# Forgetting attention in a hybrid block: token blocks handled in fours instead of pairs, row tiles of their own width, and a smaller GpSimd DMA scratch

## The chip, the cores and the metric

The kernel runs on one core of one Trainium2 chip. The metric is the device time of one execution in microseconds. The time before is 1698.5 us, the median of three runs (1698.43 to 1699.84). All arithmetic is on 32-bit floats; matrix products use the form `float32r`, in which an operand is split into a rounded high part and the rest, and one product becomes two or three matrix instructions.

## The reference, cut to what matters

One layer of a streaming encoder on 1024 tokens of width 1024: a gated linear recurrence (HGRN2), forgetting attention (FoX), cross-attention into 256 memory tokens, a gated merge, and a feed-forward mixer. The change lies in the forgetting attention alone, eight heads of 64 channels:

```python
s = (jnp.einsum('bhqd,bhkd->bhqk', qh[:, :, lo:hi], kh[:, :, :hi]) * scale
     + Fc[:, :, lo:hi, None] - Fc[:, :, None, :hi])
mask = (lo + jnp.arange(Q_BLOCK))[:, None] >= jnp.arange(hi)[None, :]
p = jax.nn.softmax(jnp.where(mask, s, -jnp.inf), axis=-1)
outs.append(jnp.einsum('bhqk,bhkd->bhqd', p, vh[:, :, :hi]))
```

Here `lo:hi` is one of eight blocks of 128 query tokens. Block `tb` looks at the `tb + 1` key blocks up to its own; its own one is masked to a triangle. `Fc` is a running sum of log forget gates.

## The kernel before, in words

The program is one long stream per engine, and its stages follow each other: input projections and gates, cross-attention, forgetting attention, HGRN2, merge, feed-forward. Python generators yield after each step, and `weave` mixes several of them by shares. The order on each engine is then fixed at build time by a planner that plays the program through on modelled times (`schedule_with_timeline_sim=True`); `ahead` raises the priority of what a generator emits by 300. On the chip each engine carries out its list in that fixed order.

**Forgetting attention** is `fox_attn` (from L901), called for each of four pairs `p` of heads and each head `i` of the pair. It is woven with work that fills TensorE meanwhile: the projection of the next pair (`fox_proj`, 256 columns a matmul) for `i = 0`, chunks of the gates (`gates_early`, 512 columns) for `i = 1`, and for the last pair HGRN2's values and then HGRN2's first projections (`hgrn_prep`). A head does its eight query blocks in four pairs `tp`:

- For each of the two blocks: two matmuls per piece of up to 512 keys into the PSUM tile `lg` (L924, L925), VectorE adds the bias and takes the row maximum (L930), ScalarE takes the exponential and its sum (L940), VectorE the reciprocal (L941), GpSimd scales the row (L942). The result is `pt`, of which there are four buffers of 1024 columns.
- Then, for two key blocks at a time, four (or three) 128x128 transposes (L953, L954, L956) fill one of two PSUM banks `tr`. `split` makes the high part `ph` on ScalarE (L166) and the rest `pl` on VectorE (L174), two buffers each. Per key block one matmul with `ph` (L965) and one with `pl` (L966) follow, both with the values `vhl` as weights, into the PSUM bank `po`, of which there is one. They have 256 columns (both query blocks), or 128 for the key block that only the second query block sees.
- At the end of a pair of blocks ScalarE copies the lower half of `po` (L969), VectorE adds the upper half (L970), and SyncE's queue writes `yp` to HBM (L971).

`fox_proj` squares its projections into `fsq` (L857 to L859), which for pairs after the first takes one of the four `pt` buffers. All these tiles are in the pool `pf`, which lies in the place of the cross-attention's pool and is followed in the same place by HGRN2's pool `ph` (`open_hgrn`).

GpSimd issues 128 DMAs in the run: some weights (`rw`, L595 and L1457), sums of weights made by accumulating DMAs (L1522, L1523), and a few others. For the descriptors of these DMAs the program reserves a scratch in each SBUF partition, whose size is a parameter of the program (L1804); where it isn't given, as here, it is 16384 bytes.

Of the kernel before, what the change touches and what calls it, by code (L numbers as in the profile page):

```python
# [8 lines left out]
F32 = mybir.dt.float32  # L9
F32R = mybir.dt.float32r  # L10
AF = mybir.ActivationFunctionType
ALU = mybir.AluOpType
AX = mybir.AxisListType

P = 128
T = 1024
D = 1024
KC = D // P
HB = 512
# [19 lines left out]
FOX_STEPS, HGRN_STEPS, MEM_STEPS = 28, 14, 7  # L39
AHEAD = 300  # L40
FOX_LATE = 0.2
SEQ = ("w0 x0 s0 w1 x1 s1 w2 x2 s2 w3 x3 s3 w4 x4 s4 x5 s5 x6 s6 x7 s7 u0 u1 u2 u3 mn u4 u5 u6 u7 lk k0 k1 k2 k3 lx "
       "q0 me k4 q1 k5 c0 ly c1 lz q2 q3 k6 q4 q5 k7 d0 q6 q7 xn d1 mv cv f1 f2 f3 du ev mk").split()
WFIRST = {0: (0, 1), 1: (1, 2), 2: (2, 3), 3: (3, 4), 4: (4, 8)}
# [47 lines left out]
def run_all(gen):  # L92
    for _ in gen:
        pass
# [15 lines left out]
def tile_block(ctx: ExitStack, tc: tile.TileContext, xT, memT, x_rows, mem_rows, vec, fbias, mats, hmask, w_first, w_cm, w_hi, w_fqk, w_fv,  # L110
               w_mkv, w_br, w_out, w_up, w_dn, w_pair, outT):
    nc = tc.nc
    V, S, G, PE, SP = nc.vector, nc.scalar, nc.gpsimd, nc.tensor, nc.sync
# [25 lines left out]
    ident = cp.tile([P, P], F32, tag="ident", name="ident")  # L139
# [24 lines left out]
    def cast(eng, out, in_):  # L164
        if eng is S:
            return S.copy(out, in_)  # L166
        elif eng is V:
            return V.tensor_copy(out, in_)
        else:
            return G.tensor_scalar(out, in_, 1.0, 0.0, ALU.mult, ALU.add)  # L170

    def split(eng, h, l, src, sub=None):
        late["split cast"] = cast(eng, h, src)
        return (sub or V).tensor_sub(l, src, h.bitcast(F32))  # L174
# [64 lines left out]
    pt = Rounded(tc, name="pt", bufs=1, side="right")  # L239
# [212 lines left out]
    ybd = tc.dram_tile([P, 4, T], F32, name="ybd")  # L452
# [165 lines left out]
    named = dict(du=first_unit, f1=families_step, f2=families_step, f3=families_step, mn=mem_norm, me=keys_out, mk=mem_keys, mv=mem_values, xn=x_norm, lk=load_late, lx=lambda: load_rows(*T2[2:], *T1[2:]), ly=lambda: load_rows(*T2[:2]), lz=lambda: load_rows(*T2[2:]), ev=first_gates, cv=first_cover)  # L618
    for what in SEQ:
        if what in named:  # L620
# [101 lines left out]
    pm = Rounded(tc, name="pm", bufs=1, side="right", reuse_waits="tile")  # L722
    pools = {}
# [120 lines left out]
    def fox_proj(p):  # L844

        fox_z[p] = [None, None]

        def evac(tb, ps):
            n, b = tb // 4, tb % 4
            if b == 0:  # L850
                fox_z[p][n] = pq.tile([P, 4, 256], F32, tag="z", name=f"z{p}_{n}", bufs=2)
            z = fox_z[p][n]
            S.activation(z[:, b, :], ps, AF.Copy, scale=rt[:, tb:tb + 1])
            if b == 3:
                zz = z.rearrange("p b (h d) -> p (b h) d", d=64)
                sq = pools["pf"].tile([P, 16, 64], F32, tag="pt", name="fsq", bufs=4) if p else \
                    pm.tile([P, 16, 64], F32, tag="fsq", name="fsq")  # L857
                r = cp.tile([P, 16], F32, tag="fr", name="fr", bufs=2)
                S.activation(sq, zz, AF.Square)  # L859
                V.reduce_sum(r, sq, axis=AX.X)  # L860
                rstd_small(r, r, 64)
                V.tensor_mul(zz, zz, r.unsqueeze(2).to_broadcast([P, 16, 64]))

        yield from token_major(w_fqk[p], 256, evac)
# [36 lines left out]
    def fox_attn(p, i):  # L901
        kh, kl, qa, _ = fox_sets[p]
        h = 2 * p + i
        a = slice(64 * i, 64 * i + 64)
        if h not in fox_vh:
            fox_vsplit(h)
        vhl = fox_vh[h]
        nf = pf.tile([P, T], F32, tag="nf", name="nf")
        SP.dma_start(nf, negFd[h:h + 1, :].partition_broadcast(P))
        for tp in range(4):  # L910
            pts = []
            for j in range(2):
                tb = 2 * tp + j
                ns = (tb + 1) * P
                tsl = slice(tb * P, (tb + 1) * P)
                pt = pf.tile([P, T], F32, tag="pt", name="pt", bufs=4)
                st = pf.tile([P, 4], F32, tag="st", name="st", bufs=4)
                nfm = pf.tile([P, P], F32, tag="nfm", name="nfm")
                G.tensor_tensor(nfm, nf[:, tsl], mskf, ALU.add)
                m = 0  # L920
                for s0 in range(0, ns, HB):
                    w = min(HB, ns - s0)
                    ps = ps_lg()
                    PE.matmul(ps[:, :w], qa[i][:, tsl], kh[i][:, s0:s0 + w], start=True, stop=False)  # L924
                    fox_sets[p][3] = PE.matmul(ps[:, :w], qa[i][:, tsl], kl[i][:, s0:s0 + w], start=False, stop=True)  # L925

                    d = w - P if s0 + w == ns else w
                    for lo, hi, bias in ((0, d, nf[:, s0:s0 + d]), (d, w, nfm)):
                        if lo < hi:
                            V.tensor_tensor_reduce(out=pt[:, s0 + lo:s0 + hi], in0=ps[:, lo:hi], in1=bias,  # L930
                                                   op0=ALU.add, op1=ALU.max, scale=1.0, scalar=-3e38,
                                                   accum_out=st[:, m:m + 1])
                            m += 1
                if m == 3:
                    V.tensor_tensor(st[:, 0:1], st[:, 0:1], st[:, 2:3], ALU.max)
                if m > 1:
                    V.tensor_scalar(st[:, 2:3], st[:, 0:1], st[:, 1:2], -1.0, ALU.max, ALU.mult)  # L937
                else:
                    V.tensor_scalar(st[:, 2:3], st[:, 0:1], -1.0, None, ALU.mult)
                S.activation(pt[:, :ns], pt[:, :ns], AF.Exp, bias=st[:, 2:3], accum_out=st[:, 3:4])  # L940
                V.reciprocal(st[:, 3:4], st[:, 3:4])  # L941
                G.tensor_scalar(pt[:, :ns], pt[:, :ns], st[:, 3:4], 0.0, ALU.mult, ALU.add)  # L942
                pts.append(pt)
                yield
            po = ps_po()
            for sp in range(tp + 1):
                ptr = ps_tr()
                w = 384 if sp == tp else 512
                for jj in range(2):
                    sb = 2 * sp + jj  # L950
                    ssl = slice(sb * P, (sb + 1) * P)
                    if sb <= 2 * tp:
                        PE.transpose(ptr[:, jj * 256:jj * 256 + P], pts[0][:, ssl], ident)  # L953
                        PE.transpose(ptr[:, jj * 256 + P:jj * 256 + 256], pts[1][:, ssl], ident)  # L954
                    else:
                        PE.transpose(ptr[:, 256:384], pts[1][:, ssl], ident)  # L956
                ph = pf.tile([P, HB], F32R, tag="ph", name="ph", bufs=2)
                pl = pf.tile([P, HB], F32R, tag="pl", name="pl", bufs=2)
                split(S, ph[:, :w], pl[:, :w], ptr[:, :w])
                for jj in range(2):  # L960
                    sb = 2 * sp + jj
                    last = sb == 2 * tp + 1
                    o = po[:, P:256] if last else po[:, 0:256]
                    src = slice(256, 384) if last else slice(jj * 256, jj * 256 + 256)
                    PE.matmul(o, vhl[:, sb, :], ph[:, src], start=(sb == 0), stop=False)  # L965
                    PE.matmul(o, vhl[:, sb, :], pl[:, src], start=False, stop=last)  # L966
                yield
            yp = pf.tile([64, 256], F32, tag="yp", name="yp")
            S.copy(yp, po[64:128, :256])  # L969
            V.tensor_add(yp, po[0:64, :256], yp)  # L970
            SP.dma_start(ybd[a, p, tp * 256:(tp + 1) * 256], yp)  # L971
            yield

    weave((chain(fox_values(), fox_proj(0)), 25), (ahead(memory(), AHEAD), 4 * MEM_STEPS))
# [1 line left out]
    pf = pools["pf"] = Rounded(tc, name="pf", bufs=1, side="right", reuse_waits="tile")  # L976
# [4 lines left out]
    for p in range(3):  # L981
        weave((ahead(fox_attn(p, 0), AHEAD), FOX_STEPS), (fox_proj(p + 1), 8))
        fox_prep(p + 1, fox_sets[p][3])
        weave((ahead(fox_attn(p, 1), AHEAD), FOX_STEPS), (gates_early(NFOX[2 * p + 1]), 2 * NFOX[2 * p + 1], FOX_LATE))

# [246 lines left out]
    for i in range(2):  # L1232
        weave((ahead(fox_attn(3, i), AHEAD), FOX_STEPS), (islice(values, 8), 8),
              (gates_early(0 if i else NFOX[6]), 2 * NFOX[6], FOX_LATE))
    run_all(values)
# [96 lines left out]
    pl = Rounded(tc, name="pl", bufs=1, side="right", reuse_waits="tile")  # L1332
# [39 lines left out]
    for i, j in enumerate((0, 4, 1, 5, 2, 6, 3, 7)):  # L1372
        chunk = cm_chunk(w_out[j], KC, mh, ml, i == 7)
        if i == 7:
            sum7 = pu.tile([P, T], F32, tag="rx", name="sum7")
            first = next(chunk)
            begun = first_operands()
            chunk = chain((first,), chunk)
        for n, ps in chunk:
# [10 lines left out]
            else:  # L1390
                sq = sqs[:, sl]
# [152 lines left out]
    for p in range(NF // 2):  # L1544
# [32 lines left out]
        for i in range(2):  # L1577
            f = 2 * p + i
            c = pq.tile([P, T], F32, tag="fc", name="fc", bufs=4)
            w = [col(C_CW + t * NF + f) for t in range(3)]  # L1580
# [88 lines left out]
    for a, b, own, first, c, n, sign, last, xq in (  # L1669
# [9 lines left out]
        for i, ks in enumerate(steps):  # L1679
# [11 lines left out]
            for m in range(4):  # L1691
# [6 lines left out]
                if ks.stop == NP:  # L1698
                    j, sl = m + 4 * c, slice(n * HB, (n + 1) * HB)
# [115 lines left out]
```

## Time and profile before

| What | Value |
|---|---|
| Median of three runs | 1698.5 us (1698.43 to 1699.84) |
| The profiled execution's own time | 1700.23 us |
| Its span in the trace | 1698.4 us |
| Granted TensorE clock | 0.999 |
| Instructions in the trace | 24291, of them 8957 matmuls |
| Forgetting attention's stage | from about 324 us to 681 us of the span |

The span reaches from the first to the last instruction of the program; the execution's own time is 1.8 us longer. In the rows below, `PE` is a matmul on TensorE, `PEld` the load of its weights, `DVE` VectorE, `ACT` ScalarE, `POOL` GpSimd. A row of groups gives a line of the kernel, the engine, the operation, output and inputs, shapes and the count, then the busy time in us and the mean duration in ns, and last the idle time before. A row of a timeline gives start and duration in us. A row of windows gives the busy time and, as (x...), the count of instructions that lie in or reach into the window.

### The profile page before, as it was taken

Reading aid. Unit: us, or ns where it says so; the run is one execution under the profiler, and the core shown is the slowest. Engines: PE = TensorE matmul, PEld = TensorE weight load, DVE = VectorE, ACT = ScalarE, POOL = GpSimd, SP = SyncE. Lnnn points to the kernel's source line nnn. Section 1 sums busy time; section 2 is a strip of 40 time slices with the busy share of each in tenths; the row PEclk is TensorE's granted clock in tenths of the full one; section 3 lists DMA queues with packets and bytes.
Section 4 is the critical chain, followed back from the end, with each engine's and each line's share of the span. In section 5 each row is a group of like instructions: output and inputs, shape, how many; then the busy total and the mean of one; then the engine's idle time right before and its main releaser. Section 6 shows DMA issues by size and latency. Waiting matters only on the chain.

```text
span 1698.4 us, 24291 instructions
## 1 busy us (share of the span) xinstructions
PE 1691.0 (100%) x8957; PEld 1452.4 (86%) x8957; DVE 1150.8 (68%) x2057; ACT 800.9 (47%) x1428; POOL 324.6 (19%) x420
## 2 busy tenths in 40 slices
PE   9999999999999999999999999999999999999999
PEld 7888899989898998888888888888888888888887
DVE  6966455666666664886856845987878888775654
ACT  6734455545454553775631333644434444533432
POOL 0200032543433331544310000311111111100000
PEclk9999999999999999999999999999999999999999
DMA  9443232221212111110346542566544344494772
GB/s 367 157 161 106 88 139 68 77 92 51 94 59 77 63 46 57 67 32 13 106 127 209 167 186 100 165 174 169 158 139 138 118 149 143 172 363 145 251 269 87
DMA packets 83062, 227.16 MB, mean 134 GB/s; under 512 B 9712, under 2 KB 12408, under 8 KB 82816
## 3 DMA queue, kind: packets, MB, share of 16 engines
q1 hardware_dynamic: 64320, 160.54, 26.8%
q0 software_dynamic: 18048, 64.50, 13.2%
q8 instruction: 70, 1.15, 0.3%
q10 hardware_dynamic: 576, 0.59, 0.1%
q14 instruction: 48, 0.39, 0.1%
HBM read 180.72 MB, written 67.93 MB: 146 GB/s over the span
## 4 chain that ended last, share of the span: by engine, by line
PE 99%; DVE 0%; ACT 0%; DMA 0%; issue 0%; ACTq 0%; DVEq 0%
PE pp L160 21%; PE pp L162 21%; PE pp L161 21%; PE lg L160 4%; PE lg L162 4%; PE lg L161 4%; PE tr L162 3%; PE tr L161 3%; PE tr L160 3%; PE po L966 1%; PE lg L925 1%; PE lg L924 1%; PE po L965 1%; PE po L160 1%; PE po L161 1%; PE po L162 1%
## 5 line engine op out<-in xcount | busy, mean ns | idle before, releaser
L160 PE MATMUL pp<-uh,wh 128*128 128x512 f32 x412 | 163.3, 396 | 0.0
L161 PE MATMUL pp<-ul,wh 128*128 128x512 f32 x412 | 162.9, 395 | 0.0
L162 PE MATMUL pp<-uh,wl 128*128 128x512 f32 x412 | 162.5, 394 | 0.0
L161 PE MATMUL pp<-wl,uh 128*128 128x256 f32 (+1 forms) x512 | 146.3, 286 | 0.0
L162 PE MATMUL pp<-wh,ul 128*128 128x256 f32 (+1 forms) x512 | 146.1, 286 | 0.0
L160 PE MATMUL pp<-wh,uh 128*128 128x256 f32 (+1 forms) x512 | 145.6, 286 | 0.0
L166 ACT CAST wh<-s 128x512 fp32r<-128x512 f32 x110 | 66.5, 621 | 131.6 <-PE pp L161 55.1
L166 ACT CAST wh<-raw 128x1024 fp32r<-128x1024 f32 (+2 forms) x76 | 67.6, 890 | 100.6 <-PE pp L161 86.2
L166 ACT CAST wh<-rw 128x512 fp32r<-128x512 f32 x87 | 53.2, 619 | 108.1 <-PE pp L161 70.2
L160 PEld LDWEIGHTS pp<-wh,uh 128*128 128x128 f32 x512 | 97.3, 190 | 1.2
L161 PEld LDWEIGHTS pp<-wl,uh 128*128 128x128 f32 x512 | 97.4, 190 | 1.0
L162 PEld LDWEIGHTS pp<-wh,ul 128*128 128x128 f32 x512 | 97.4, 190 | 0.9
L1457 POOL DMA_DIRECT2D rw<-in_w_up x44 | 24.1, 555 | 372.4 <-DVE wl L1350 171.3
L166 ACT CAST dwh<-wr 128x1024 fp32r<-128x1024 f32 (+1 forms) x41 | 40.2, 980 | 115.8 <-PE tr L161 40.0
L162 PEld LDWEIGHTS pp<-uh,wl 128*128 128x128 f32 x412 | 77.5, 188 | 15.1
L174 DVE TENSOR_TENSOR wl<-raw,wh 128x1024 fp32r<-128x1024 f32 (+2 forms) x75 | 78.0, 1040 | 17.8 <-ACT wh L166 17.6
L160 PEld LDWEIGHTS pp<-uh,wh 128*128 128x128 f32 x412 | 77.5, 188 | 14.6
L161 PEld LDWEIGHTS pp<-ul,wh 128*128 128x128 f32 x412 | 77.5, 188 | 14.5
L940 ACT ACTIVATE pt<-pt,st 128x128 f32<-128x128 f32 (+3 forms) x64 | 49.7, 777 | 41.7 <-DVE st L937 33.9
L174 DVE TENSOR_TENSOR dwl<-wr,dwh 128x1024 fp32r<-128x1024 f32 (+1 forms) x41 | 46.3, 1129 | 31.7 <-ACT dwh L166 31.7
L942 POOL TENSOR_SCALAR pt<-pt,st 128x128 f32<-128x128 f32 (+3 forms) x64 | 49.1, 767 | 78.4 <-DVE st L941 64.1
L1350 DVE TENSOR_TENSOR wl<-rw,wh 128x512 fp32r<-128x512 f32 x69 | 47.7, 704 | 22.7 <-PE pp L162 18.2
(500 smaller groups left out, 5123.2 us busy)
## 6 DMA issues: line engine op xcount, KB each, us to landing
rw<-in_w_up POOLq DMA_DIRECT2D x44, 512.0 KB, 4.7
sd<-in_w_dn POOLq DMA_DIRECT2D x30, 512.0 KB, 6.0
br<-yd SPq DMA_DIRECT2D x30, 512.0 KB, 5.0
raw<-in_w_cm SPq DMA_DIRECT2D x24, 512.0 KB, 3.4
gd<-gt SPq DMA_DIRECT2D x48, 256.0 KB, 2.0
gt<-gd SPq DMA_DIRECT2D x48, 256.0 KB, 2.7
yd<-fc SPq DMA_DIRECT2D x44, 256.0 KB, 2.2
wr<-sd SPq DMA_DIRECT2D x20, 512.0 KB, 4.5
```

The costliest lines, as they stand in the source:

```text
L160: PE.matmul(ps, lh, rh, start=first, stop=False, skip_group_check=more)
L161: PE.matmul(ps, lh, rl, start=False, stop=False, skip_group_check=more)
L162: return PE.matmul(ps, ll, rh, start=False, stop=last, skip_group_check=more)
L166: return S.copy(out, in_)
L174: return (sub or V).tensor_sub(l, src, h.bitcast(F32))
L924: PE.matmul(ps[:, :w], qa[i][:, tsl], kh[i][:, s0:s0 + w], start=True, stop=False)
L925: fox_sets[p][3] = PE.matmul(ps[:, :w], qa[i][:, tsl], kl[i][:, s0:s0 + w], start=False, stop=True)
L940: S.activation(pt[:, :ns], pt[:, :ns], AF.Exp, bias=st[:, 2:3], accum_out=st[:, 3:4])
L942: G.tensor_scalar(pt[:, :ns], pt[:, :ns], st[:, 3:4], 0.0, ALU.mult, ALU.add)
L965: PE.matmul(o, vhl[:, sb, :], ph[:, src], start=(sb == 0), stop=False)
L1350: late["split"] = V.tensor_sub(l, src, h.bitcast(F32))
L1457: late["raw"] = G.dma_start(raw[:, 2 * i:2 * i + 2, :], src[:, 2 * i:2 * i + 2, :])
```

## The change

A head does its eight query blocks in two groups `g` of four. The rows of the eight blocks get eight tiles `pt0` to `pt7`, each of the width that the block needs (128 to 1024 columns, one buffer each), in place of four buffers of 1024. For one key block at a time, up to four transposes fill a PSUM bank, one for each query block of the group that sees this key block; one split and two matmuls of 512, 384, 256 or 128 columns follow. `ph` and `pl` have three buffers (`PARTS`). The end of a group copies and adds 512 columns. `fsq` gets a tile of its own. GpSimd's DMA scratch is set to 4096 bytes.

```diff
-                sq = pools["pf"].tile([P, 16, 64], F32, tag="pt", name="fsq", bufs=4) if p else \
-                    pm.tile([P, 16, 64], F32, tag="fsq", name="fsq")
+                sq = (pools["pf"] if p else pm).tile([P, 16, 64], F32, tag="fsq", name="fsq")
...
-        for tp in range(4):
+        for g in range(2):
             pts = []
-            for j in range(2):
-                tb = 2 * tp + j
+            for tb in range(4 * g, 4 * g + 4):
...
-                pt = pf.tile([P, T], F32, tag="pt", name="pt", bufs=4)
+                pt = pf.tile([P, ns], F32, tag=f"pt{tb}", name=f"pt{tb}")
...
             po = ps_po()
-            for sp in range(tp + 1):
+            for sb in range(4 * g + 4):
                 ptr = ps_tr()
-                w = 384 if sp == tp else 512
-                for jj in range(2):
-                    sb = 2 * sp + jj
-                    ssl = slice(sb * P, (sb + 1) * P)
-                    if sb <= 2 * tp:
-                        PE.transpose(ptr[:, jj * 256:jj * 256 + P], pts[0][:, ssl], ident)
-                        PE.transpose(ptr[:, jj * 256 + P:jj * 256 + 256], pts[1][:, ssl], ident)
-                    else:
-                        PE.transpose(ptr[:, 256:384], pts[1][:, ssl], ident)
-                ph = pf.tile([P, HB], F32R, tag="ph", name="ph", bufs=2)
-                pl = pf.tile([P, HB], F32R, tag="pl", name="pl", bufs=2)
-                split(S, ph[:, :w], pl[:, :w], ptr[:, :w])
-                for jj in range(2):
-                    sb = 2 * sp + jj
-                    last = sb == 2 * tp + 1
-                    o = po[:, P:256] if last else po[:, 0:256]
-                    src = slice(256, 384) if last else slice(jj * 256, jj * 256 + 256)
-                    PE.matmul(o, vhl[:, sb, :], ph[:, src], start=(sb == 0), stop=False)
-                    PE.matmul(o, vhl[:, sb, :], pl[:, src], start=False, stop=last)
+                first = max(sb - 4 * g, 0)
+                for j in range(first, 4):
+                    PE.transpose(ptr[:, j * P:(j + 1) * P], pts[j][:, sb * P:(sb + 1) * P], ident)
+                ph = pf.tile([P, HB], F32R, tag="ph", name="ph", bufs=PARTS)
+                pl = pf.tile([P, HB], F32R, tag="pl", name="pl", bufs=PARTS)
+                c = slice(first * P, HB)
+                split(S, ph[:, c], pl[:, c], ptr[:, c])
+                PE.matmul(po[:, c], vhl[:, sb, :], ph[:, c], start=sb == 0, stop=False)
+                PE.matmul(po[:, c], vhl[:, sb, :], pl[:, c], start=False, stop=sb == 4 * g + 3)
                 yield
...
-    nc = bacc.Bacc("TRN2", target_bir_lowering=False, num_devices=1)
+    nc = bacc.Bacc("TRN2", target_bir_lowering=False, num_devices=1, dynamic_dma_scratch_size=4096)
```

More of the change, by code (lines that the diff above doesn't have):

```diff
@@ L41 @@
 FOX_LATE = 0.2
+PARTS = 3
 SEQ = ("w0 x0 s0 w1 x1 s1 w2 x2 s2 w3 x3 s3 w4 x4 s4 x5 s5 x6 s6 x7 s7 u0 u1 u2 u3 mn u4 u5 u6 u7 lk k0 k1 k2 k3 lx "
@@ L939, in fox_attn @@
                     V.tensor_scalar(st[:, 2:3], st[:, 0:1], -1.0, None, ALU.mult)
-                S.activation(pt[:, :ns], pt[:, :ns], AF.Exp, bias=st[:, 2:3], accum_out=st[:, 3:4])
+                S.activation(pt, pt, AF.Exp, bias=st[:, 2:3], accum_out=st[:, 3:4])
                 V.reciprocal(st[:, 3:4], st[:, 3:4])
-                G.tensor_scalar(pt[:, :ns], pt[:, :ns], st[:, 3:4], 0.0, ALU.mult, ALU.add)
+                G.tensor_scalar(pt, pt, st[:, 3:4], 0.0, ALU.mult, ALU.add)
                 pts.append(pt)
@@ L967, in fox_attn @@
+                PE.matmul(po[:, c], vhl[:, sb, :], pl[:, c], start=False, stop=sb == 4 * g + 3)
                 yield
[L968 to L971, printed above, removed]
+            yp = pf.tile([64, HB], F32, tag="yp", name="yp")
+            S.copy(yp, po[64:128, :])
+            V.tensor_add(yp, po[0:64, :], yp)
+            SP.dma_start(ybd[a, p, g * HB:(g + 1) * HB], yp)
```

## The prediction

> **What bounds the kernel now.** I read the page's busy times first, then the chain of work that ended last.
>
> ```profile
> span 1698.4 us, 24291 instructions
> PE 1691.0 (100%) x8957; PEld 1452.4 (86%) x8957; DVE 1150.8 (68%) x2057; ACT 800.9 (47%) x1428; POOL 324.6 (19%) x420
> ...
> PE 99%; DVE 0%; ACT 0%; DMA 0%; issue 0%; ACTq 0%; DVEq 0%
> ```
>
> TensorE is busy all through, and the chain lies on it to 99%. But the page warns that the ends of matmuls are modelled. So I read the groups by form, then starts in the timeline.
>
> ```profile
> L161 PE MATMUL pp<-wl,uh 128*128 128x256 f32 x448 | 127.9, 286 | 0.0
> L161 PE MATMUL pp<-ul,wh 128*128 128x512 f32 x211 | 83.4, 395 | 0.0
> ...
> 343.40 0.34 PE L924 MATMUL lg<-kh,qa 128*128 128x384 f32 x1
> 343.57 0.34 PE L925 MATMUL lg<-kl,qa 128*128 128x384 f32 x1
> 343.75 0.28 PE L160 MATMUL pp<-wh,uh 128*128 128x256 f32 x1
> 343.87 0.28 PE L161 MATMUL pp<-wl,uh 128*128 128x256 f32 x1
> ...
> 652.14 0.28 PE L966 MATMUL po<-pl,vhl 128*128 128x256 f32 x1
> 652.26 0.22 PE L965 MATMUL po<-ph,vhl 128*128 128x128 f32 x1
> 652.32 0.28 PE L966 MATMUL po<-pl,vhl 128*128 128x128 f32 x1
> 652.43 0.45 PE L161 MATMUL pp<-ul,wh 128*128 128x512 f32 x1
> ```
>
> A matmul of 256 columns "lasts" 286 ns, yet the next one starts 0.12 us after it. What TensorE pays is the distance from start to start, which I call the pitch: 0.175 us at 384 columns (343.40, 343.57, 343.75), 0.17 us for two of 128 (652.26 to 652.43). For 512 and 256 columns I take windows in which TensorE does nothing else.
>
> ```profile
> 1200.00:1300.00 100.00, 100.00 (x442) 82.78 (x442) 81.87 (x121) 43.51 (x66) 12.38 (x20) 1.00 0.48 139
> 320.00:326.00 6.00, 6.00 (x53) 6.00 (x52) 4.63 (x6) 2.67 (x5) 5.66 (x6) 1.00 0.40 145
> 324.00:685.00 361.00, 361.00 (x2381) 329.55 (x2381) 220.21 (x656) 184.24 (x360) 127.47 (x174) 1.00 0.19 65
> ```
>
> The second column is TensorE. In each count some two matmuls began before the window: 100 / 440 = 0.227 us at 512 columns, 6 / 51 = 0.118 us at 256. So columns cost nearly alike in any shape; a matmul of its own costs about 0.009 us beside them (2 x 0.118 - 0.227).
>
> The third window is forgetting attention. Does TensorE wait there? I price its contents by pitch.
>
> ```profile
> L162 PE MATMUL pp<-wh,ul 128*128 128x256 f32 x298 | 85.0, 286 | 0.0
> L966 PE MATMUL po<-pl,vhl 128*128 128x256 f32 x128 | 34.7, 293 | 0.0
> L924 PE MATMUL lg<-kh,qa 128*128 128x512 f32 x48 | 20.4, 425 | 0.0
> L953 PE MATMUL tr<-ident,pt 128*128 128x128 f32 x128 | 32.1, 276 | 0.0
> L966 PE MATMUL po<-pl,vhl 128*128 128x128 f32 x32 | 8.9, 278 | 0.0
> ...
> 644.57 0.27 PE L953 MATMUL tr<-ident,pt 128*128 128x128 f32 x1
> 644.68 0.27 PE L956 MATMUL tr<-ident,pt 128*128 128x128 f32 x1
> 644.79 0.27 PE L954 MATMUL tr<-ident,pt 128*128 128x128 f32 x1
> ```
>
> With its sisters each kind counts: 892 filler matmuls of 256 columns (105.3 us), 633 of 512 (143.7), the products with the values (256 x 0.118 + 32 pairs x 0.17 = 35.6), the scores (96 x 0.227 for 512 columns and 12 us for the smaller ones, 33.9), 288 transposes of rows at 0.11 us and 56 of projections (37.8). That is 356 us of 361: **waits make up at most 5 us of the stage**. TensorE itself is the bound; VectorE has 220 of 361 us, ScalarE 184.
>
> **The change part by part.**
>
> *The products with the values.* Before, a head has 32 matmuls of 256 columns and 8 of 128 (256 and 64 in all). After, group 0 has key blocks seen by 4, 3, 2 and 1 query blocks, group 1 four more seen by 4: in all 12 matmuls of 512, 4 of 384, 4 of 256, 4 of 128. Both are 9216 columns. By pitch: before 32 x 0.118 + 4 x 0.17 = 4.46 us, after 12 x 0.227 + 4 x 0.175 + 4 x 0.118 + 2 x 0.17 = 4.24 us. That is 0.22 us a head, **1.8 us** in eight heads; with the 256-column pitch anywhere in 0.117 to 0.120, 1.5 to 2.2. TensorE is saturated, so this gain reaches the end. The transposes stay 36 a head, and the scores are untouched.
>
> The Trainium skill, TensorE: Matmul & The Clock Gate, section "Back-to-back issue gap", gives N/2.4 + 2.5 ns for isolated matmuls of N columns. By that, 16 matmuls less a head would save 16 x 8 x 2.5 ns = 0.3 us (an estimate from that page); the windows here show 0.227 us at 512 columns where it gives 0.216, so the trace's own pitches stand in the sum.
>
> *The splits.* ScalarE and VectorE split the same columns in more pieces.
>
> ```profile
> L166 ACT CAST ph<-tr 128x512 fp32r<-128x512 f32 x48 | 27.1, 588 | 24.9 <-PE tr L954 16.9 <-PE po L965 7.4
> L174 DVE TENSOR_TENSOR pl<-tr,ph 128x512 fp32r<-128x512 f32 x48 | 32.2, 684 | 12.0 <-ACT ph L166 11.8
> L174 DVE TENSOR_TENSOR pl<-tr,ph 128x384 fp32r<-128x384 f32 x32 | 17.6, 549 | 1.4 <-ACT ph L166 1.3
> L970 DVE TENSOR_TENSOR yp<-po,yp 64x256 f32<-64x256 f32 x32 | 13.2, 412 | 13.1 <-ACT yp L969 12.9
> L969 ACT COPY yp<-po 64x256 f32<-64x256 f32 x32 | 11.8, 369 | 31.9 <-PE po L966 31.5
> ```
>
> Six of 512 and four of 384 become six of 512 and two each of 384, 256 and 128. 128 columns are 0.135 us of VectorE, so that is two fixed parts of about 0.14 us more a head; against it two `yp` additions fall away (4 x 0.412 against 2 x 0.68). VectorE and ScalarE change by under 0.4 us a head and each has over 140 us free in the stage: nothing, hidden behind TensorE. Were that cover gone, 8 x 0.4 = 3 us. SyncE's queue writes two `yp` a head in place of four.
>
> *Own row tiles.* The next head's block `tb` waits until this head's has been transposed; with four shared buffers it waited for the block four back. `nf` and `po` keep one buffer. I count nothing either way.
>
> *The wait that grows.* No product of a group can begin until its fourth block is scaled, where it was the second. The waiting instructions stand in TensorE's fixed order; behind them stand all fillers. What covers it are fillers ahead of them. Bounds: gain, the 5 us of waits; loss, see the third rival. I take zero, since nearly nothing waits there now.
>
> *Smaller scratch.* GpSimd's DMAs are 18048 packets.
>
> ```profile
> q0 software_dynamic: 18048, 64.50, 13.2%
> ...
> 1435.23 0.56 POOL L1457 DMA_DIRECT2D rw<-in_w_up  x1 [11.20 <-DVE wl L1350]
> 1436.97 0.54 POOL L1457 DMA_DIRECT2D rw<-in_w_up  x1 [1.18 <-issue]
> ...
> 1302.02 1.09 POOL L1457 DMA_DIRECT2D rw<-in_w_up  x2 [10.65 <-DVE wl L1350]
> ...
> 1313.85 0.62 ACT L166 CAST wh<-rw 128x512 fp32r<-128x512 f32 x1 [2.03 <-issue]
> ...
> rw<-in_w_up POOLq DMA_DIRECT2D x44, 512.0 KB, 4.7
> ```
>
> 128 issues make 18048 / 128 / 16 = 8.8 packets per issue on each of 16 engines. Once, between the 113th and the 114th issue, GpSimd stood 1.18 us with nothing to wait for in the profile. If that is the scratch beginning again, a quarter of it does so four times, some 5 us of GpSimd, each beside weights that have slack: those issued at 1302.02 are first cast at 1313.85, and the last row gives 4.7 us to landing. Nothing; if that cover is missing, up to 4 x 1.2 us.
>
> The Trainium skill, DMA: Bandwidth & Descriptors, section "SWDGE vs HWDGE vs iDMA", says GpSimd appends descriptors to rings in an SBUF carve-out, and its first table gives 16 bytes each. An estimate from this page: 256 places a ring in place of 1024, and the 114th issue would be the one to pass 1024. No run here shows what a full ring costs.
>
> **The sum.** 1698.4 - 1.8 = 1696.6 us of span. The profiled execution's own time was 1700.2, so it would be 1698.4; the median of the runs shown was 1.7 us lower, and there the same 1.8 us gives **1696.7 us**, with 1694.5 to 1699 as this case's own range (2.2 and a little of the waits below, 0.5 above for the fixed order being drawn anew).
>
> **The rivals.**
>
> *Busy times are prices.* By the groups' means 256 columns are 0.29 us, 512 are 0.39 and 128 are 0.28: 32 x 0.29 + 8 x 0.28 - (12 x 0.39 + 4 x 0.34 + 4 x 0.29 + 4 x 0.28) = 3.2 us a head, 26 us in all, 1673 us. Against it: starts lie 0.12 us apart. The Trainium skill's page Perfetto Trace Analysis calls matmul busy time a bad metric because matmuls are pipelined, and the trace agrees. Chance 0.03.
>
> *The waits shrink too.* Three buffers of `ph` and `pl`, larger pieces, `fsq` out of the rows' places: the 5 us of waits go as well, and HGRN2's stage behind begins better placed.
>
> ```profile
> 685.00:900.00 215.00, 214.24 (x1226) 181.95 (x1225) 160.25 (x264) 126.01 (x303) 78.87 (x71) 1.00 0.25 81
> ```
>
> There the count is thin for the time, so waits lie there that a new order can move. Gain 1.8 + 2 to 6, likeliest 4: 1693 us. Chance 0.25.
>
> *The last head's tail (slower).* Its last row is scaled by 661.4; then come the outcome steps, and what follows in `pf`'s place waits for them.
>
> ```profile
> 660.25 1.12 POOL L942 TENSOR_SCALAR pt<-pt,st 128x1024 f32<-128x1024 f32 x1 [6.18 <-PE tr L956]
> ...
> 673.46 0.97 ACT L166 CAST ph<-tr 128x512 fp32r<-128x512 f32 x2 [2.92 <-PE tr L954]
> ...
> 680.08 0.37 ACT L969 COPY yp<-po 64x256 f32<-64x256 f32 x1 [5.65 <-PE po L966]
> 680.35 0.63 ACT L1048 ACTIVATE ha<-gt 128x512 f32<-128x512 f32 x1
> ```
>
> Two splits a round, a round every 6 to 7 us with filler matmuls between: after 661 two rounds before, four after (eight key blocks). The tail then ends near 687 to 693, and HGRN2's first tile `ha` with it. It decides when the fillers are used up: three PSUM banks and three gate tiles hold six half chunks of 24 x 0.227 = 5.4 us, 33 us in all, some of it used by 661. Beyond that TensorE waits: one or two rounds' 6 us, less the 1.8. At 6 us net, 1704 us. For it: the eight steps; against it: the margin of some 6 us. The same mechanism in any earlier head finds gates to fill with. Chance 0.2.
>
> *The scratch holds weights back.* 4 x 1.2 us less 1.8: 1701.5 us. Chance 0.02.
>
> **How the numbers follow.** The forecast has 0.5. A measurement of this kernel can tell 0.2%, 3.4 us, from no change: faster is below 1695.1, slower above 1701.9. Faster: the first two rivals (0.28, a part of the second lies inside 0.2%) and the lowest edge of the forecast, 0.3. Slower: most of the tail's 0.2 and a part of the scratch, 0.21. Same: 0.49. The range takes the second rival's and the tail's prices with their bounds and leaves out the first and the worst tail: 1690 to 1705.
>
> **What would show it.** L965 and L966 with 96 matmuls each, 512 columns among them at a pitch of 0.227. The stage from the first score to the last `yp` addition shorter by about 2 us. GpSimd's idle time at DMA issues marked "issue", four places where one was, with no TensorE wait behind. `ha` on ScalarE no later than about 690, with the windows from 661 to 700 as full as now. I am wrong if the windows behind 685 hold the difference, or if forgetting attention's stage gains over 5 us.

## The result, and the profile after

The changed kernel is slower: 1718.2 us median of 4 runs (1717.63 to 1720.62), against 1699.17 us (1698.43 to 1700.18) for the kernel before, a ratio of 1.0114 with a 95% interval of 1.0097 to 1.0132. The profiled execution took 1718.75 us, its span is 1717.0. So some 19 us were lost where 1.8 were to be gained. First the page of the kernel after:

```profile
span 1717.0 us, 23916 instructions
PE 1694.5 (99%) x8829; PEld 1448.5 (84%) x8829; DVE 1150.9 (67%) x2057; ACT 798.3 (46%) x1428; POOL 319.7 (19%) x420
...
PE 94%; DVE 2%; ACT 2%; DMA 2%; issue 0%; ACTq 0%; SPq 0%; DVEq 0%
```

The 128 matmuls fewer are there (8957 less 8829), but the span less TensorE's busy time was 7.4 us and is 22.5, and the chain of work that ended last now has VectorE, ScalarE and DMA in it. Where TensorE waits is told by the view of waits from 640 to 960 us of the kernel after (waiting line, what it waited for, us in total, times, longest):

```profile
PE pp L161 <- DVE gt L1282: 8.2, 1, 8.2
PE pp L161 <- DVE gt L1035: 3.0, 1, 3.0
PE tr L1163 <- DVE kE L1155: 2.9, 1, 2.9
...
```

In the kernel before, the same view has one wait, of 0.7 us. The view of windows puts them in their places; behind a window's length stands TensorE's busy time, the last column but two is the granted clock, the last but one the DMA share. In the kernel before TensorE is busy all through each of the windows named here, as in these two:

```profile
660.00:685.00 25.00, 25.00 (x133) 21.35 (x132) 8.33 (x16) 7.78 (x14) 5.96 (x5) 1.00 0.18 59
...
900.00:950.00 50.00, 50.00 (x222) 41.39 (x221) 34.15 (x54) 9.19 (x15) 0.00 (x0) 1.00 0.52 165
```

In the kernel after:

```profile
660.00:685.00 25.00, 23.04 (x113) 19.07 (x112) 7.29 (x12) 6.28 (x11) 1.25 (x3) 1.00 0.08 27
685.00:700.00 15.00, 12.32 (x47) 9.79 (x47) 9.62 (x16) 7.49 (x13) 5.25 (x4) 0.89 0.38 122
700.00:720.00 20.00, 18.82 (x99) 15.66 (x100) 15.06 (x22) 17.39 (x45) 11.39 (x9) 0.91 0.07 27
...
900.00:950.00 50.00, 41.83 (x178) 33.99 (x177) 24.40 (x37) 4.79 (x8) 0.00 (x0) 0.93 0.72 259
```

To turn this into a ledger I gave every matmul of either trace the pitch of its shape (0.227 us for 512 columns, 0.119 for 256, 0.174 for 384, 0.11 for a transpose, and so on) and added up what is still to be done at a given time. The totals hang on these prices; only the differences are used:

| Matmul time left at | before | after | after less before |
|---|---|---|---|
| 324 us | 1350.7 | 1348.6 | -2.1 |
| 600 us | 1077.7 | 1075.7 | -2.0 |
| 640 us | 1038.1 | 1038.1 | 0.0 |
| 660 us | 1018.4 | 1018.3 | -0.1 |
| 685 us | 993.6 | 995.6 | +2.0 |
| 700 us | 978.6 | 984.9 | +6.3 |
| 720 us | 960.2 | 968.8 | +8.6 |
| 900 us | 793.7 | 802.1 | +8.4 |
| 950 us | 743.5 | 762.2 | +18.7 |

At 324 us the kernel after has 2.1 us less to do. That much is arithmetic, counts times pitches. What the trace adds is that up to 600 us both kernels work off the same, 273.0 and 272.9 us, so the wide matmuls of this stretch cost what their pitch says and nothing is lost. Then come three losses: **2.0 us** between 600 and 640, **8.7 us** between 660 and 720, **10.3 us** between 900 and 950, 21.0 in all. Less the 2.1 that makes 18.9; the span grew by 18.6.

**The loss at 900.** It lies some 220 us behind the last instruction that the forgetting attention has. The chain of work that ended last, from 895 to 925 us of the kernel after (start, us, what):

```profile
901.72 8.66 DMA x<-in_xT
...
910.44 9.97 DMA gt<-gd
...
920.43 0.70 DVE gt L1282
```

TensorE waits until VectorE has multiplied an earlier product of the merge by a gate, and the gate was being fetched for 10 us. The row of DMA issues gives 2.7 us as the median of these loads (48 of 256 KB). What lay ahead of it is seen in the timeline of SyncE's queue, of after and then of before:

```profile
901.72 6.41 SPq L1325 DMA_DIRECT2D x<-in_xT  x8
910.44 0.33 SPq L1275 DMA_DIRECT2D gt<-gd  x1
```

```profile
977.18 3.99 SPq L1336 DMA_DIRECT2D x<-in_xT  x8
```

Eight loads of 512 KB, the tiles `x1` of the stage behind the merge, are issued at 902 us in place of 977. They stand ahead of gate loads that are needed at once: the load at 910.44 is the next one that SyncE issues. Of the 10.3 us, 8.2 are the wait; some 1.5 more come from a low clock behind it, of which the last section has the row.

**The loss at 683.** TensorE's timeline of after, around the last product with the values:

```profile
682.76 0.28 PE L955 MATMUL po<-pl,vhl 128*128 128x128 f32 x1
685.99 0.79 PE L161 MATMUL pp<-uh,wh 128*128 128x512 f32 x1 [2.95 <-DVE gt L1035]
686.59 0.63 PE L162 MATMUL pp<-ul,wh 128*128 128x512 f32 x1
687.01 0.63 PE L163 MATMUL pp<-uh,wl 128*128 128x512 f32 x1
```

The next filler has no PSUM bank: the banks wait for evacuations (L1035, the multiplication of a projection by `rx`) that stand on VectorE behind the `yp` addition:

```profile
684.66 0.68 DVE L959 TENSOR_TENSOR yp<-po,yp 64x512 f32<-64x512 f32 x1
685.27 1.27 DVE L1035 TENSOR_TENSOR gt<-pp,rx 128x512 f32<-128x512 f32 x2
```

How it came to this is in the `ph` casts of the last head, on ScalarE's timeline of after:

```profile
658.83 1.08 ACT L167 CAST ph<-tr 128x512 fp32r<-128x512 f32 x2 [0.26 <-PE tr L949]
666.02 1.07 ACT L167 CAST ph<-tr 128x512 fp32r<-128x512 f32 x2 [6.12 <-PE tr L949]
...
672.25 0.59 ACT L167 CAST ph<-tr 128x512 fp32r<-128x512 f32 x1 [2.56 <-PE tr L949]
673.28 0.48 ACT L167 CAST ph<-tr 128x384 fp32r<-128x384 f32 x1 [0.44 <-PE tr L949]
678.53 0.56 ACT L167 CAST ph<-tr 128x256 fp32r<-128x256 f32 x2 [4.77 <-PE tr L949]
```

All eight key blocks of the last group come behind its last softmax row. They go in four rounds of two, one for each of the two `tr` banks, some 6.5 us apart, with fillers between. The kernel before has three rounds there, the third at 673.46:

```profile
660.50 0.48 ACT L166 CAST ph<-tr 128x384 fp32r<-128x384 f32 x1 [0.61 <-PE po L965]
...
666.65 1.08 ACT L166 CAST ph<-tr 128x512 fp32r<-128x512 f32 x2
```

Its last product ends at 680 and fillers go on. In the kernel after it ends at 683, and no filler has a bank to go on with. Of the 8.7 us, 2.95 are this wait, 2.9 a second one that begins at 698 us, for `kE` of HGRN2's chain. After the first wait TensorE runs at half pace for a while: in the rows above matmuls start 0.43 us apart in place of 0.227. The clock is low behind the second wait too; the two stretches, some 1.5 us each, make up most of the rest.

**The loss at 614** is 2 us in small waits (the waits of 0.26, 0.21 and 0.39 us are its largest) and in matmuls that start further apart than their pitch. I come to it with the experiments.

### The profile page after: what moved, and what is told of

It is laid out like the page before. It is cut to its first block, busy times and chain, and to the rows that moved or that the text cites. A ratio compares the mean times of both kernels' runs of the same rounds, so it can differ in the third digit from the quotient of the medians.

```text
span 1717.0 us, 23916 instructions
## 1 busy us (share of the span) xinstructions
PE 1694.5 (99%) x8829; PEld 1448.5 (84%) x8829; DVE 1150.9 (67%) x2057; ACT 798.3 (46%) x1428; POOL 319.7 (19%) x420
## 4 chain that ended last, share of the span: by engine, by line
PE 94%; DVE 2%; ACT 2%; DMA 2%; issue 0%; ACTq 0%; SPq 0%; DVEq 0%
PE pp L161 20%; PE pp L163 20%; PE pp L162 20%; PE lg L161 4%; PE lg L162 4%; PE lg L163 4%; PE tr L161 3%; PE tr L162 3%; PE tr L163 3%; PE tr L949 2%; PE po L955 1%; PE lg L924 1%; PE po L161 1%; PE lg L923 1%; PE po L954 1%; PE po L162 1%
## 5 line engine op out<-in xcount | busy, mean ns | idle before, releaser
L167 ACT CAST ph<-tr 128x512 fp32r<-128x512 f32 (+1 forms) x96 | 43.6, 478 | 86.3 <-PE tr L949 85.9
L175 DVE TENSOR_TENSOR pl<-tr,ph 128x512 fp32r<-128x512 f32 (+1 forms) x96 | 51.4, 552 | 36.1 <-ACT ph L167 35.9
```

## The experiments

My theory: the two large losses have separate causes. The scratch brings the `x1` loads forward, because 12288 bytes more lie free in each partition and `x1` gets places that nothing of the merge still reads; the groups of four make the last head's tail too long. The rivals: that the smaller descriptor ring slows GpSimd's DMAs, and that the early `x1` loads only follow from the delay at 683.

**1. The `x1` loads held back.** The kernel after, with the eight loads ordered behind the last gate load.

```diff
-                SP.dma_start(gt, gd[i, n])
+                late["gate load"] = SP.dma_start(gt, gd[i, n])
...
     for j in range(8):
-        SP.dma_start(x1[j], xT[:, j, :])
+        with tc.issue_after(late["gate load"].ins):
+            SP.dma_start(x1[j], xT[:, j, :])
```

> The changed kernel, with the eight loads of the residual input (x1) held on SyncE's queue behind the last gate load (gt) of the merge. Main theory: the trace of after shows two separate losses, about 10.5 us around 600 to 720 us (the last head's tail) and about 10 us at 912 to 921 us, where TensorE waits for a gate product whose gt load stands behind the eight x1 loads on SyncE's queue; so this gives back about 10 us, 1718 to about 1708. Rival (the smaller scratch itself slows GpSimd's DMAs, or the DMA engines were full anyway): the wait at 912 stays, 1716 to 1718.

Measured: 1708.87 us against 1700.09, ratio 1.0047 [1.0032, 1.0062]. The window from 900 to 950 is full again (50.00), the wait at 683 stays. Half the loss hangs on the place of eight loads in a queue. It acts in two ways: the gate load that went out at 910.44 us and took 10.0 us to land now goes out at 905.86 and takes 4.4.

**2. The small scratch alone,** in the kernel before.

```diff
-    nc = bacc.Bacc("TRN2", target_bir_lowering=False, num_devices=1)
+    nc = bacc.Bacc("TRN2", target_bir_lowering=False, num_devices=1, dynamic_dma_scratch_size=4096)
```

> The kernel before, with nothing changed but the scratch of GpSimd's DMAs, 4096 bytes in place of 16384. Main theory: 12288 bytes more of SBUF lie between the tiles that grow from its two ends, so the places of x1 no longer lie on tiles that are read until the merge ends; the x1 loads are queued some 75 us earlier, ahead of gate loads, and TensorE waits about 8 us as in after: 1699 to about 1709, the stretch before 880 us unchanged. Rival (the scratch is harmless, all of the loss comes from the blocks in fours): 1699.

Measured: 1710.09 us, ratio 1.0057 [1.0042, 1.0072]. Nothing of the attention is changed, and the loss is there; its queue and its one large wait:

```profile
892.01 6.40 SPq L1336 DMA_DIRECT2D x<-in_xT  x8
```

```profile
PE pp L160 <- DVE gt L1293: 8.5, 1, 8.5
```

So the delay at 683 is no condition of it.

**3. The small scratch, and its free bytes taken up** by a tile that nothing uses.

```diff
+    cp.tile([P, 3072], F32, tag="hole", name="hole")
     ngx = cp.tile([P, 4], F32, tag="ngx", name="ngx")
...
-    nc = bacc.Bacc("TRN2", target_bir_lowering=False, num_devices=1)
+    nc = bacc.Bacc("TRN2", target_bir_lowering=False, num_devices=1, dynamic_dma_scratch_size=4096)
```

> The kernel before with the scratch at 4096 bytes and an unused tile of 12288 bytes behind it, so that every other tile lies where it lay before and the order of the queues stays. Main theory: 1699, no change, since the scratch acts through the places alone. Rival (fewer descriptors hold GpSimd's DMAs back): as slow as the kernel with the small scratch alone, over 1703, with waits behind the weights that GpSimd loads.

Measured: 1700.4 us, ratio 0.9999 [0.999, 1.0009]. The loads are back in their old place:

```profile
978.31 3.96 SPq L1337 DMA_DIRECT2D x<-in_xT  x8
```

The ring of a quarter of the size costs nothing that these runs can tell. Nor does GpSimd stand still at its DMA issues in four places, which the prediction had among its signs. The stall of 1.18 us at the 114th issue is gone,

```profile
1436.65 1.09 POOL L1458 DMA_DIRECT2D rw<-in_w_up  x2 [11.41 <-DVE wl L1351]
```

and the longest that is marked "issue" is 0.67 us, at the 50th issue, where the kernel before has one of 0.38. What the 1.18 us was stays open; that the ring began again there is not borne out. With experiments 1, 2 and 3 the cause of the 10 us is shown: the bytes that came free, by way of the order of SyncE's queue. Which tile's place had kept `x1` back was not traced.

**4. The last head in pairs.** The kernel after, with the old loop (and the new tiles) for head seven alone.

```diff
+        if h == 7:
+            for tp in range(4):
...
+            return
         for g in range(2):
```

> The changed kernel, with the last of the eight heads done in pairs of blocks as before (its row tiles stay of their own width, its splits have three buffers). Main theory: the eight steps after the last head's last row are the cause of the loss at 600 to 720 us; four rounds become two or three, and about 8 to 10 us come back: about 1709, with the 8 us wait at 912 still there. Rival (the new places of the tiles, on which HGRN2's tiles now wait, are the cause): the gap at 683 us stays, 1716 to 1718.

Measured: 1711.03 us, ratio 1.0061 [1.0046, 1.0076]. No wait is left between 660 and 720 us, and 8.1 us for the gate `gt` remain. The loss at 683 comes from one head of eight.

**5. Both: loads held back, last head in pairs.**

> The changed kernel with both remedies: x1 loads held behind the last gate load, and the last head in pairs. Main theory: the two losses add up and both go; what is left is the 1.8 us gain of wider products (seven heads) less some 2 us that TensorE waits at 611 to 617 us in head six: 1700 to 1701, the same as before. Rival (the remedies overlap, or a third loss is hidden behind them): 1703 or more.

Measured: 1700.68 us against 1700.25, ratio 1.0000 [0.9992, 1.0009]. The two causes account for the whole loss against the kernel before. Against experiment 1 the tail costs 8 us (0.0047 of 1700).

**6. Places and buffers without the fours:** loads held back, all heads in pairs, but with tiles of their own width, three `ph` and `pl`, and the small scratch.

```diff
-        for g in range(2):
+        for tp in range(4):
...
                 pt = pf.tile([P, ns], F32, tag=f"pt{tb}", name=f"pt{tb}")
```

> The changed kernel, x1 loads held, but all eight heads in pairs of blocks: row tiles of their own width, own place for the squares, three buffers for the splits, small scratch. Main theory: the places cost nothing, 1700, TensorE as full at 600 to 720 us as before. Rival (HGRN2's tiles wait on the new places): a gap near 683 us stays, 1703 to 1709.

Measured: 1701.23 us, ratio 1.0005 [0.9996, 1.0014]; one of the eleven runs took 8257 us, for a reason not known, and the ratio leaves it out. The new places of the rows and the third buffers do no harm and bring nothing that these runs can tell.

**7. The last head's groups in the other order,** the one of four key blocks last. If the steps behind the last row are what counts, four steps in place of eight should mend it.

```diff
-        for g in range(2):
+        for g in (1, 0) if h == 7 else (0, 1):
```

> The changed kernel, x1 loads held, the last head in fours but with its second group (blocks 4 to 7, eight steps) ahead of its first (blocks 0 to 3, four steps). Main theory: what counts is how many steps follow the last row; four in place of eight bring back most of the tail's loss: 1700 to 1703, against 1708.9 with the x1 loads held alone. Rival (any group of four in the last head is too coarse for what lies behind it): 1707 to 1709.

Measured: 1711.12 us, ratio 1.0063 [1.0051, 1.0076]. **This was wrong.** ScalarE's timeline shows the twelve steps of both groups one behind the other, from 657 us on, and the last ones late:

```profile
657.28 1.08 ACT L167 CAST ph<-tr 128x512 fp32r<-128x512 f32 x2 [0.94 <-PE tr L949]
...
670.84 0.97 ACT L167 CAST ph<-tr 128x512 fp32r<-128x512 f32 x2 [3.41 <-PE tr L949]
...
685.52 0.27 ACT L167 CAST ph<-tr 128x128 fp32r<-128x128 f32 x1 [1.53 <-PE tr L949]
686.68 0.58 ACT L958 COPY yp<-po 64x512 f32<-64x512 f32 x1 [0.89 <-PE po L955]
```

The longer group's rows come first here, but its steps don't start earlier than 657. I read from this that what counts is not the row behind which a step stands but how many steps are left when the rounds begin, and their pace. The pace is tested in experiment 9.

**8. Heads six and seven in pairs,** loads held back, to take out the loss at 614, where I held the fours of head six responsible.

```diff
-        if h == 7:
+        if p == 3:
```

(against the kernel of experiment 5)

> The changed kernel, x1 loads held, with both heads of the last pair of heads in pairs of blocks and the first six heads in fours. Main theory: the wait at 611 to 617 us goes too, and the six heads keep 6 x 0.22 = 1.3 us: 1698.5 to 1699.5 beside 1700.1 before. Rival (the wider products give nothing on the chip): 1700 or more.

Measured: 1700.93 us, ratio 1.0006 [0.9997, 1.0014]. **Wrong as well.** The wait stays, and in it a row that names another cause:

```profile
616.65 0.39 PE L161 MATMUL pp<-wh,uh 128*128 128x256 f32 x1 [0.55 <-ACT Vf L1069]
```

The filler here is HGRN2's values `Vf`, evacuated into the place of the attention's `Vf`. The half of that place that heads four to seven use is read until the last head's `vhl` is made from it (from 610.4 us before, 615.9 after, 615.4 here). `vhl` has two buffers, so the last head's waits until the products of the head two before it are done, and these end later in fours. So the theory became: no filler can stand in this stretch, whatever head six does. It fits that TensorE is busy all through from 600 to 640 us in experiment 6, where that head too is in pairs.

**9. Four banks for the last group of the last head,** loads held back: every second step takes a bank of `lg`, which has no more rows to compute. This is the test of the pace.

```diff
-                ptr = ps_tr()
+                ptr = ps_lg() if h == 7 and g and sb % 2 else ps_tr()
```

> The changed kernel, x1 loads held; in the last head's second group every other step puts its transposes into a bank of the scores (lg), which are done by then, so that three steps (three split buffers) instead of two (two tr banks) can be under way. Theory of the pace: in the tail TensorE's order has two steps, then about 22 filler matmuls (5 us), then the next two; the fillers run out at the eighth step. With three steps a round the tail takes three rounds in place of four and the gap at 683 us goes: 1700 to 1703 against 1708.9 with the x1 loads held alone. Rival (something else than the banks spaces the steps): 1707 to 1709.

Measured: 1700.19 us against 1698.99, ratio 1.0002 [0.9993, 1.0010]; against experiment 1 some 8 us better, with the fours kept in every head. The casts of the second group take from 656.9 to 669 us (658.8 to 679 in the kernel after), and `yp` is copied 9 us earlier than in the kernel after (there at 683.51):

```profile
656.91 0.59 ACT L167 CAST ph<-tr 128x512 fp32r<-128x512 f32 x1
657.40 0.59 ACT L167 CAST ph<-lg 128x512 fp32r<-128x512 f32 x1
...
668.97 0.27 ACT L167 CAST ph<-lg 128x128 fp32r<-128x128 f32 x1 [2.03 <-PE po L954]
...
674.34 0.58 ACT L958 COPY yp<-po 64x512 f32<-64x512 f32 x1 [3.63 <-PE po L955]
```

That settles the second cause: eight steps at two a round, a bank being what a round lacks. (The planner draws the whole order anew for each edit, so each of these experiments changes the order of the fillers too.)

**10. Two buffers of `ph` and `pl`,** loads held back.

```diff
-PARTS = 3
+PARTS = 2
```

> The changed kernel, x1 loads held, with two buffers for the splits in place of three. Theory of the pace: two tr banks allow two steps a round whatever the split buffers: no change from 1708.9, within 1.5. Rival (the third buffer is in use, and the tail would be longer without it): 1711 or more.

Measured: 1710.08 us, ratio 1.0063 [1.0047, 1.0078]; its interval overlaps that of experiment 1. The tail's wait of 2.95 us is the same with two buffers; the third is no part of it.

**11. Three tiles `vhl`,** on the kernel of experiment 9, with `fsq` in the place of `pt7` to make room.

```diff
-tag="vhl", name="vhl", bufs=2)
+tag="vhl", name="vhl", bufs=3)
```

> The kernel with four banks in the last head's tail and the x1 loads held, and a third place for the split values (vhl), paid for by putting the squares (fsq) into the place of the widest row. Theory: the 2 us lost at 609 to 617 us come from HGRN2's values, whose evacuation into Vf waits until the last head's vhl has been made from it, and that waits for head five's outcome, which ends later in fours; with a third place vhl is made earlier, TensorE has fillers there, and about 2 us come back: 1697 to 1698 where the kernel before takes 1699 to 1700, a ratio near 0.9988. Rival (the wait is on the scores or rows themselves): no change, ratio 1.000.

Measured: 1699.28 us against 1700.07, ratio 0.9997 [0.9989, 1.0006]. The last `vhl` is made at 568.0 us, the waits at 614 are gone, and the ledger at 640 us has 1034.5 us left against 1036.8 in experiment 9: the 2 us are back, by this cause. But waits of 0.6 us each on HGRN2's `X` (L1087 and L1121) come up at 698 and 708 us, and at 950 us 0.5 us of the 2.3 remain. The median can't tell it from the kernel before.

**12. The same on the kernel of experiment 5.**

> The kernel with both remedies (x1 loads held, last head in pairs) and the same third place for the split values. Same theory: about 2 us less than with two places, ratio near 0.999 to the kernel before. Rival: ratio 1.000 as with two places.

Measured: 1701.98 us, ratio 1.0014 [1.0005, 1.0023]. **Wrong in sign.** The waits at 614 are gone here too, but TensorE stands still later:

```profile
680.60 0.40 PE L163 MATMUL pp<-uh,wl 128*128 128x512 f32 x1
683.76 0.50 PE L161 MATMUL pp<-uh,wh 128*128 128x512 f32 x1 [2.76 <-DVE gt L1100]
684.09 0.40 PE L162 MATMUL pp<-ul,wh 128*128 128x512 f32 x1
```

It waits for the same evacuation as the kernel after at 683: the fillers done early at 614 are missing here. That is read from the rows; I did not test it.

No version beats the kernel before by more than can be told; experiment 11 comes nearest.

## Why the prediction was wrong

*TensorE as the bound and the pitch: right, as far as the rows go.* The products with the values are 192 matmuls of the right widths, and two of 512 columns in a row start 0.23 us apart:

```profile
664.36 0.39 PE L955 MATMUL po<-pl,vhl 128*128 128x512 f32 x1
664.59 0.39 PE L954 MATMUL po<-ph,vhl 128*128 128x512 f32 x1
```

The gain is 2.0 to 2.1 us in the ledger, predicted were 1.8; the ledger takes 0.119 us for 256 columns where the prediction takes 0.118. No run shows it in the time: no version is faster than the kernel before by more than can be told. The rival that took busy times as prices (26 us) is out.

*The splits, own row tiles, `fsq`, third buffers: right within what the runs can tell.* They were costed at nothing. Experiment 6 puts places and buffers between 0.7 us of gain and 2.4 us of loss, and experiment 9, with the splits in fours in every head, is at 1.0002.

*"Smaller scratch … Nothing": the first step that failed, and the largest,* 10 us of 19. I asked what a smaller ring does to the DMAs that use it, found slack and a price of 4 x 1.2 us without it, and experiment 3 bears that out: a ring of 4096 bytes costs nothing that can be told. (The estimate that the 114th issue would pass 1024 places does not follow from its own figure: 114 x 8.8 is 1003.) But a smaller scratch is also 12288 bytes that go to the tiles. I never asked who gets them. They let `x1` be loaded 75 us earlier, on the queue that also brings the gates. The profile of before held what was needed to ask: `x<-in_xT` x8 of 512 KB in its row of DMA issues, and a DMA share of 52% from 900 to 950 us. It could not have shown that the planner would put the loads ahead of the gates.

*"The wait that grows … I take zero": the second step that failed.* The case stands among the rivals as the last head's tail, with its mechanism: two splits a round, four rounds, fillers used up, at 6 us net and a chance of 0.2. Its net size in experiment 1 is 8 us [5.4, 10.5], at 0.0047 of 1700. What I got wrong was the argument against it, "the margin of some 6 us": TensorE ran dry at 683, 3 us behind the end of the kernel before's last product and earlier than the tail's end at 687 to 693 that I had asked for. Of the two signs that I had set for it, one held with the loss there (`ha` began at 684.00, in time for "no later than about 690"); the other, windows from 661 to 700 as full as before, told it. And the price of running dry is more than the wait: 2.95 us of it, a second wait of 2.9 us in HGRN2's chain, and a stretch at a low clock behind each. Experiments 4 and 9 remove it, once by fewer steps, once by more banks.

*What no step had:* the 2 us at 614, where the outcome of a head that ends later holds `vhl`, and through it the place of the fillers. Experiment 11 shows this cause. In the ledger it takes the whole gain of the pitch, and experiment 5 comes out at the time before. That without it the gain would reach the end is not shown: where it is taken away, experiment 11 loses most of the 2 us again later, and experiment 12 more than that.

*The rival "The waits shrink too"* did not happen. The prediction's own sign of being wrong did: the windows behind 685 hold most of the difference.

Open: why the planner sets the rounds some 6.5 us apart; which tile's place had kept `x1` back; and what it is in experiment 11's redrawn order that loses most of the 2 us again behind 690.

## What to carry to other kernels

Memory that comes free is a change of order: ask which later tile may now be loaded earlier, on which queue, and which urgent transfer stands behind it; a tile that nothing uses, put into the free place, tells the two effects of such an edit apart. A coarser group cost nothing here up to 600 us, where other work fills in, so price it where fillers end: steps left behind the last row, divided by the banks that a round has, against the fillers that are still there. And where TensorE is full all through, the start-to-start distance is the price, and merging matmuls of equal columns was worth 0.1% here, which one wait of 3 us takes back.

## What the runs showed of the hardware that was not expected

A wait of TensorE can cost more than its length. In the windows of 3 us of the kernel after, behind its waits that end at 686, 701 and 921 us, the granted clock (last column but two) falls and comes back:

```profile
686.00:689.00 3.00, 3.00 (x7) 2.42 (x8) 0.54 (x1) 1.20 (x2) 2.90 (x3) 0.50 0.87 292
689.00:692.00 3.00, 3.00 (x14) 2.48 (x14) 2.77 (x6) 0.00 (x0) 1.34 (x2) 1.00 0.12 44
...
701.00:704.00 3.00, 2.82 (x12) 2.39 (x13) 1.71 (x4) 3.00 (x12) 2.28 (x2) 0.77 0.00 0
704.00:707.00 3.00, 3.00 (x15) 2.49 (x13) 3.00 (x5) 2.98 (x7) 2.78 (x3) 0.66 0.00 0
921.00:924.00 3.00, 2.73 (x7) 2.19 (x8) 2.93 (x6) 0.62 (x1) 0.00 (x0) 0.50 0.60 208
```

Seven matmuls in place of fourteen in the first: 1.5 us more for a wait of 2.95. In experiment 12 a wait of 2.76 us left the clock at 1.00 (the starts above, 0.33 and then 0.24 us apart). In experiment 7 a much shorter one was enough; its window from 683 to 686 us has a clock of 0.62, and 0.79 us is how long the first matmul behind the wait of the kernel after took, too:

```profile
683.14 0.44 PE L949 MATMUL tr<-ident,pt 128*128 128x128 f32 x2 [1.58 <-DVE pl L175]
683.73 0.79 PE L954 MATMUL po<-ph,vhl 128*128 128x512 f32 x1 [0.15 <-DVE yp L959]
```

Ahead of that wait TensorE had only transposes for 0.5 us, and behind it two more; from the end of the last product (681.22) to the next (683.73) it is 2.5 us. Whether transposes count as work for the clock, no run here shows; 2.5 is still less than the 2.76 of experiment 12.

The Trainium skill, TensorE: Matmul & The Clock Gate, section "Why this matters for your kernels", says that one idle window drops the clock to half, and advises against gaps over about 3 us. The waits of 2.95 and 2.76 us agree with a limit near there; the 1.58 us of experiment 7 do not, and the measurement decides: the length of a wait alone does not tell. The page's Part 1 calls the window in which idleness is judged free-running, by which waits of like length may end differently; no run here shows that.

And a load of 256 KB took 10.0 us where its kind has a median of 2.7, with 4 MB issued ahead of it on the same queue from 8.7 us before; without these the same load took 4.4 us (experiment 1). Bulk loads of this kind are not the only thing that makes it slow: in the kernel before, the two gate loads issued at 887.8 and 888.4 us took 8.1 and 9.5 us.
